# Channel shuffle of 64 MiB: loads and stores in turn on one DMA queue in place of a queue for each

## The chip, the cores and the metric

One core of a Trainium2 chip runs the kernel; the other cores are idle. The metric is the device time of one execution in microseconds (us), median over fast runs. Ratios are from the fast runs of both kernels in the same rounds, so not quite the ratio of the medians quoted. The experiments came in three groups, each on one chip with its own runs of the kernel before (medians 317.56, 317.75 and 316.95 us); compare within a group, and between groups by these ratios only. In the third group the seven runs of the kernel before fall into two sets, 316.8 to 317.0 and 317.6 to 317.9 us, so a ratio of that group is uncertain by some 0.2%.

## The reference

```python
# x: (16, 64, 64, 256) float32, groups = 8, 32 channels in each
x = x.reshape(batch, h, w, groups, channels_per_group)
x = x.transpose(0, 1, 2, 4, 3)
x = x.reshape(batch, h, w, c)
```

Each row of 256 floats is permuted in itself. 67.11 MB are read and 67.11 MB are written; there is no arithmetic.

## The kernel before

```python
_SIZES = [4, 4, 8] + [24] * 20 + [16]     # rows per partition of each tile, 1 KB a row
_IN_BUFS = 4
_OUT_BUFS = 4
...
    for q in _SIZES:
        in_tile = in_pool.tile([P, biggest * c], F32, name="in_tile")
        nc.sync.dma_start(out=in_tile[:, : q * c], in_=rows(x_flat, first, q))
        out_tile = out_pool.tile([P, biggest * c], F32, name="out_tile")
        nc.vector.tensor_copy(
            out=out_tile[:, : q * c].rearrange("p (i j g) -> p i j g", j=CPG, g=G),
            in_=in_tile[:, : q * c].rearrange("p (i g j) -> p i j g", g=G, j=CPG),
        )
        nc.scalar.dma_start(out=rows(out_flat, first, q), in_=out_tile[:, : q * c])
        first += P * q
```

Twenty-four tiles go through four input and four output buffers. SyncE issues all loads on its queue, VectorE copies each tile with the channels permuted, and ScalarE issues all stores on its own queue. Most tiles have 24 KB in each of 128 partitions, 3.146 MB.

Of the kernel before, what the change touches and what calls it, by code (L numbers as in the profile page):

```python
# [1 line left out]

# [4 lines left out]


F32 = mybir.dt.float32
P = 128  # L10

_SIZES = [4, 4, 8] + [24] * 20 + [16]
_IN_BUFS = 4
_OUT_BUFS = 4


@with_exitstack
def kernel(
    ctx: ExitStack,
    tc: tile.TileContext,  # L20
    x: bass.AP,
    groups: bass.AP,
    out: bass.AP,
):
    nc = tc.nc
    b, h, w, c = x.shape
    G = int(groups)
    CPG = c // G
    assert G * CPG == c
    assert sum(_SIZES) * P == b * h * w  # L30
    biggest = max(_SIZES)

    x_flat = x.rearrange("b h w c -> (b h w c)")
    out_flat = out.rearrange("b h w c -> (b h w c)")

    in_pool = ctx.enter_context(tc.tile_pool(name="in_pool", bufs=_IN_BUFS))
    out_pool = ctx.enter_context(tc.tile_pool(name="out_pool", bufs=_OUT_BUFS))

    def rows(flat, first, q):

        return flat[first * c : (first + P * q) * c].rearrange("(p f) -> p f", p=P)

    ctx.enter_context(tc.manual_schedule(engines=None))
    first = 0
    for q in _SIZES:
        in_tile = in_pool.tile([P, biggest * c], F32, name="in_tile")
        nc.sync.dma_start(out=in_tile[:, : q * c], in_=rows(x_flat, first, q))
        out_tile = out_pool.tile([P, biggest * c], F32, name="out_tile")
        nc.vector.tensor_copy(  # L49
            out=out_tile[:, : q * c].rearrange("p (i j g) -> p i j g", j=CPG, g=G),  # L50
            in_=in_tile[:, : q * c].rearrange("p (i g j) -> p i j g", g=G, j=CPG),
        )
        nc.scalar.dma_start(out=rows(out_flat, first, q), in_=out_tile[:, : q * c])
        first += P * q


# [1 line left out]
_INS = ['x', 'groups']  # L58
_OUTS = [((16, 64, 64, 256), 'float32')]

_NUMBERS = {'groups': 8}


# [26 lines left out]
```

## Time and profile before

| | before |
|---|---|
| time, median | 317.67 us (317.63 to 317.87) |
| span of the profiled run | 315.2 us |
| VectorE busy | 122.2 us, 39% |
| queue q1 (loads), share of 16 engines' span | 49.9% |
| queue q10 (stores) | 49.5% |

How to read it: the two queue rows are shares of the time of the same 16 DMA engines, so they add up to 99.4%. The lines are shown in the prediction. Two more lines of the page:

```profile
GB/s 316 399 458 407 423 424 446 430 421 446 437 415 446 437 418 443 440 415 443 440 415 443 443 412 443 446 409 443 446 415 437 446 415 437 443 420 431 431 437 319
...
HBM read 67.11 MB, written 67.11 MB: 426 GB/s over the span
```

The first line is the rate in 40 equal slices of 7.9 us. (The profiled execution of this kernel was a quick one: it took 317.02 us.)

### The profile page before, as it was taken

To read this page: it belongs to the slowest core of one execution; us is meant where nothing else is said; L and a number is where in the kernel's file an instruction comes from. 1 tells how busy PE (TensorE), PEld (TensorE's weight loads), DVE (VectorE), ACT (ScalarE), POOL (GpSimd) and SP (SyncE) were. 2 spreads that over 40 slices of the span, in tenths; PEclk is the share of its full clock that TensorE was granted. 3 is DMA by queue.
4 is the path that set the end of the run, shared out by engine and by line. 5 is a ranking of instruction groups with operands and counts; after the bars stand their busy time and mean duration, and the time that the engine had idled before them with its cause. 6 is when DMAs were issued, how large, how long until landed. Compare 5 with 4: busy or idle time off the path is not lost.

```text
span 315.2 us, 178 instructions
## 1 busy us (share of the span) xinstructions
DVE 122.2 (39%) x24; POOL 0.2 (0%) x4
## 2 busy tenths in 40 slices
DVE  2277517070625335260707162442517070625400
POOL 0000000000000000000000000000000000000000
DMA  8999999999999999999999999999999999999997
GB/s 316 399 458 407 423 424 446 430 421 446 437 415 446 437 418 443 440 415 443 440 415 443 443 412 443 446 409 443 446 415 437 446 415 437 443 420 431 431 437 319
DMA packets 6912, 134.22 MB, mean 426 GB/s; under 512 B 768, under 2 KB 768, under 8 KB 1280
## 3 DMA queue, kind: packets, MB, share of 16 engines
q1 hardware_dynamic: 3456, 67.11, 49.9%
q10 hardware_dynamic: 3456, 67.11, 49.5%
HBM read 67.11 MB, written 67.11 MB: 426 GB/s over the span
## 4 chain that ended last, share of the span: by engine, by line
DMA 38%; another core or an unknown queue 30%; DVE 25%; issue 0%; DVEq 0%
DMA in_tile<-in_x_dram 38%; DVE out_tile L49 25%; DVEq L49 0%
## 5 line engine op out<-in xcount | busy, mean ns | idle before, releaser
L49 DVE COPY out_tile<-in_tile 128x6144 f32<-128x6144 f32 (+3 forms) x24 | 122.2, 5093 | 175.9 <-DMA in_tile<-in_x_dram 175.7
L71 POOL MEMSET const-bfloat16-1.0<- 128x1 bf16 x1 | 0.1, 101 | 0.0
L71 POOL MEMSET const-uint8-127<- 128x1 uint8 x1 | 0.1, 101 | 0.0
L71 POOL MEMSET const-float32-0.0<- 128x1 f32 x1 | 0.1, 98 | 0.2 <-issue 0.2
L71 POOL MEMSET const-float32-1.0<- 128x1 f32 x1 | 0.1, 98 | 0.0
## 6 DMA issues: line engine op xcount, KB each, us to landing
in_tile<-in_x_dram SPq DMA_DIRECT2D x20, 3072.0 KB, 52.3
out_dram<-out_tile ACTq DMA_DIRECT2D x20, 3072.0 KB, 40.1
in_tile<-in_x_dram SPq DMA_DIRECT2D x1, 2048.0 KB, 49.9
out_dram<-out_tile ACTq DMA_DIRECT2D x1, 2048.0 KB, 16.3
in_tile<-in_x_dram SPq DMA_DIRECT2D x2, 512.0 KB, 3.8
in_tile<-in_x_dram SPq DMA_DIRECT2D x1, 1024.0 KB, 6.2
out_dram<-out_tile ACTq DMA_DIRECT2D x2, 512.0 KB, 16.8
out_dram<-out_tile ACTq DMA_DIRECT2D x1, 1024.0 KB, 27.1
```

The lines of the kernel that those rows point to most:

```text
L49: nc.vector.tensor_copy(out=out_tile[:, : q * c].rearrange("p (i j g) -> p i j g", j=CPG, g=G), in_=in_tile[:, : q * c].rearrange("p (i g ...
L71: nc = _bacc.Bacc("TRN2", target_bir_lowering=False, num_devices=1)
```

## The change

The intent: keep the DMA engines fed from one queue in an exact order, store of tile t and then load of tile t + 4, so that ScalarE is free. The tile sizes and the copies stay. The diff, cut to its core:

```diff
-        nc.sync.dma_start(out=in_tile[:, : q * c], in_=rows(x_flat, first, q))
+    def load(t):
+        q = _SIZES[t]
+        in_tiles[t] = in_pool.tile([P, biggest * c], F32, name="in_tile")
+        nc.sync.dma_start(
+            out=in_tiles[t][:, : q * c], in_=rows(x_flat, firsts[t], q)
+        )
+
+    for t in range(_IN_BUFS):
+        load(t)
+    for t, q in enumerate(_SIZES):
 ...  (tensor_copy as before)
-        nc.scalar.dma_start(out=rows(out_flat, first, q), in_=out_tile[:, : q * c])
-        first += P * q
+        nc.sync.dma_start(
+            out=rows(out_flat, firsts[t], q), in_=out_tile[:, : q * c]
+        )
+        if t + _IN_BUFS < len(_SIZES):
+            load(t + _IN_BUFS)
```

More of the change, by code (lines that the diff above doesn't have):

```diff
@@ L43 @@
     ctx.enter_context(tc.manual_schedule(engines=None))
-    first = 0
-    for q in _SIZES:
-        in_tile = in_pool.tile([P, biggest * c], F32, name="in_tile")
-        nc.sync.dma_start(out=in_tile[:, : q * c], in_=rows(x_flat, first, q))
+    firsts = [P * sum(_SIZES[:t]) for t in range(len(_SIZES))]
+    in_tiles = {}
+    def load(t):
[7 more added lines that the diff above has]
+    for t, q in enumerate(_SIZES):
+        in_tile = in_tiles.pop(t)
         out_tile = out_pool.tile([P, biggest * c], F32, name="out_tile")
```

## The prediction

> **What bounds the kernel now.** I read the page in this order: engine shares, the DMA row of the 40 slices, the queues, the costliest groups, the DMA issues. The first three already name the limit.
>
> ```profile
> DVE 122.2 (39%) x24; POOL 0.2 (0%) x4
> ...
> DMA  8999999999999999999999999999999999999997
> ...
> DMA packets 6912, 134.22 MB, mean 426 GB/s; under 512 B 768, under 2 KB 768, under 8 KB 1280
> ...
> q1 hardware_dynamic: 3456, 67.11, 49.9%
> q10 hardware_dynamic: 3456, 67.11, 49.5%
> ```
>
> VectorE, the only engine that computes, works 39% of the 315.2 us span. The 16 DMA engines are busy in every slice; loads (q1, issued by SyncE) and stores (q10, issued by ScalarE) together take 49.9 + 49.5 = 99.4% of their time. So there is no idle DMA time to win, only a different rate per byte. I asked for that rate in stretches (columns: stretch, length, engines' busy time, clock, DMA share, GB/s):
>
> ```profile
> 4.00:6.00 2.00, 1.74 (x2) 0.00 (x0) 1.00 1.05 428
> ...
> 60.00:90.00 30.00, 11.42 (x2) 0.00 (x0) 1.00 1.00 433
> 100.00:200.00 100.00, 39.40 (x7) 0.00 (x0) 1.00 1.00 433
> 306.00:312.00 6.00, 0.00 (x0) 0.00 (x0) 1.00 1.01 431
> ```
>
> From 60 to 200 us both queues run and the rate is 433 GB/s. At 4 to 6 us only loads have started (one queue), at 306 to 312 us only stores are left (the other queue): 428 and 431. Thus **one queue alone, in one direction, fills all 16 engines**; a second queue adds no rate. (Stretches of 2 us are uncertain by some per cent, as packets are booked whole.)
>
> The packet records of the trace say the same: a 24,576-byte packet takes 912 ns, the median on q1 and on q10 alike. Sixteen engines at 24,576 B per 912 ns make 431 GB/s. The completion packets of 4 bytes take 9 ns each. In the store-only end the records show all 16 engines at work across the borders between stores.
>
> The floor: sum the packets by their usual times, 5120 x 912 ns + 512 x 159 (4 KB) + 256 x 309 (8 KB) + 256 x 611 (16 KB) + 768 x 9 = 4993 us; over 16 engines 312.1 us. The first packet starts 2.0 us into the span and the last ends at 314.3 us: 312.4 us of work. The kernel stands on its floor; the measured median of 317.67 is 2.5 us above the span and is taken as fixed.
>
> Now the slack of the copies and the timing of the queue:
>
> ```profile
> 0.73 243.81 SPq L47 DMA_DIRECT2D in_tile<-in_x_dram  x24
> ...
> 209.35 5.67 DVE L49 COPY out_tile<-in_tile 128x6144 f32<-128x6144 f32 x1 [8.82 <-DMA in_tile<-in_x_dram]
> 223.89 5.72 DVE L49 COPY out_tile<-in_tile 128x6144 f32<-128x6144 f32 x1 [8.87 <-DMA in_tile<-in_x_dram]
> ...
> 294.24 3.86 DVE L49 COPY out_tile<-in_tile 128x4096 f32<-128x4096 f32 x1 [6.47 <-DMA in_tile<-in_x_dram]
> ```
>
> Copies start 14.54 us apart (223.89 - 209.35), take 5.7, and wait 8.8 for a load. 14.54 us is two 3.146 MB transfers at 433 GB/s (7.27 us each): the pace is DMA bandwidth, not the copy. Section 6 of the page adds the backlog:
>
> ```profile
> in_tile<-in_x_dram SPq DMA_DIRECT2D x20, 3072.0 KB, 52.3
> out_dram<-out_tile ACTq DMA_DIRECT2D x20, 3072.0 KB, 40.1
> ```
>
> A load lands 52.3 us after its issue, 3.6 periods: transfers sit in the queue long before they run. The chain of waits also names "another core or an unknown queue" for 30%; these pieces of 8.7 us lie exactly where the next load is awaited, so I read them as loads too.
>
> **What the Trainium skill says.** "DMA: Bandwidth & Descriptors", section "Issuing engines are not separate DMA queues": DMAs started by different engines run on the same 16 DMA engines and interleave; several issuers save only issue time. The trace agrees (433 with two queues, 431 with one). Its section "Where 436 GB/s comes from" puts a ceiling of 435 GB/s at the SBUF ports and says that for HBM transfers some 358 GB/s bind; here 433 is held for hundreds of microseconds, so this trace agrees with the first and not the second. Its section "Queues, rings and completion order" says each DMA engine takes turns between its queues packet by packet, and that within a queue descriptors start in order. The records fit: from 60 us on q1 and q10 each have about half of the packets in any stretch.
>
> **The change, part by part.**
>
> 1. *Stores leave ScalarE's queue.* 24 issues of 0.36 us (median 361 ns) go away there. ScalarE does nothing else: worth 0.
>
> 2. *SyncE issues 48 DMAs in place of 24.* At 328 ns each, 2 x 0.33 = 0.66 us per 14.54 us period, while the backlog is tens of us: 0 on the path, except that in the pair (store t, load t+4) the load is issued 0.33 us later than now. Also hidden.
>
> 3. *SyncE waits for copy t before store t, so load t+4 sits behind that wait.* With 4 input buffers, load t+4 writes the buffer that copy t reads, so it had to wait for copy t already. Nothing new.
>
> 4. *The queue becomes first in, first out:* ... S(t-4), L(t), S(t-3), L(t+1), S(t-2), L(t+2), S(t-1), L(t+3), then S(t), L(t+4). When L(t) lands, six transfers are behind it: 6 x 7.27 = 43.6 us. Copy t takes 5.7 us, then two more are added. Lowest backlog: 43.6 - 5.7 = **about 38 us, the queue never runs dry**. Output buffers: copy t needs S(t-4), which stands ahead of L(t), so it is done. Start: when L3 lands near 15 us, S0, L4, S1, L5, S2, L6 (11.5 MB, 26.6 us) are queued, and copy 3 needs 5.7. End: after L23, S20 to S22 (9.44 MB, 21.8 us) remain while copy 23 needs 3.9. No gap at either end.
>
> 5. *Alternation.* Now each DMA engine changes direction at nearly every packet and still does 912 ns per packet. On one queue it changes every 8 packets (128 rows over 16 engines). About 40 changes in place of several hundred: if a change had a price, the kernel before would pay it more often. I put 0 to +0.5 us for what this argument may miss.
>
> 6. *Bytes, packet sizes, copies:* unchanged.
>
> Sum: 0 + 0 + 0 + 0 + about 0.2, so 317.67 becomes about **317.8 us**.
>
> **The rivals.**
>
> A. *The direction change inside one queue has a price.* With two queues, the other's packet can fill any hole while a completion waits for its data; in one queue the load behind a store cannot be overtaken. Same-direction borders show no hole (store-only end, 431 GB/s), but a border between store and load within one queue occurs nowhere in this trace. Being 2% (6.4 us) slower needs 6.4 / 40 = 0.16 us of hole per change on all engines. At 0.05 us it makes 319.7; at 0.3, 330. I give this most of what is left.
>
> B. *Loads win a head start.* Now small stores share turns with big loads at the start; in order, a load has all engines for 7.3 us. L23 then lands with 9.44 + 2.10 MB = 11.5 MB still to write (26.6 us), so its copy starts near 287 us rather than at 294.24. But it only exchanges store time for load time; all bytes still pass at 433. Worth 0. A real gain would need the head (2.0 us), the tail (0.9) or the some 0.3 us over the floor: 1% in all, so faster by 2% is nearly excluded.
>
> C. *The queue's depth runs out.* Up to 8 transfers, 8 x 9 = 72 packets per engine counting completions, wait in one queue where q1 now has four loads (36). If it cannot hold them, SyncE blocks on issue. Against a loss: even half the entries are over 20 us of work. It would show as long issues, not as time.
>
> **Range and chances.** Runs agree within 0.1% (317.63 to 317.87). Downward I allow the head's loss, some 1.3 us: 316.4. Upward 0.09 us per change, 40 x 0.09 = 3.5 us: 321.3. Slower by over 2% needs rival A at nearly twice that: 0.06. Faster by 2% (below 311.3) would lie under the floor of 312.1 plus the head: 0.01. Within 2%: 0.93.
>
> **What would show it.** One queue with all 134.22 MB at about 99% of the 16 engines; 433 GB/s from 60 to 280 us; copies still 14.54 us apart with 8.8 us of idle before each. From issue to landing: a load is issued 5.75 us after L(t) landed and lands 4 periods after it, 58.2 - 5.75 = 52.4 us, as now; a store lands one transfer earlier, 45.1 us (now 40.1). Last copy near 287 us. If the rate falls below 433 with the queue never dry and the period grows beyond 14.6 us, rival A is true and step 5 was wrong; if DVE idles on output buffers, or the DMA row shows slices below 9 in the middle, step 4 was wrong; if issues take microseconds, rival C.

## The result, and the profile after

The changed kernel takes **321.24 us** (320.20 to 321.51, 4 runs) against 317.76 us for the kernel before in the same rounds. The ratio is 1.0107 (95% interval 1.0087 to 1.0128): 1.1% slower, clear of noise, but within 2%. The profiled span went from 315.2 to 319.4 us.

The page of the changed kernel, the lines that answer to those of before:

```profile
DVE 121.7 (38%) x24; POOL 0.2 (0%) x4
...
GB/s 293 366 444 429 442 412 440 428 443 428 419 437 440 434 422 431 431 443 428 419 434 437 437 422 422 443 440 428 419 437 437 443 416 431 437 428 432 437 428 173
...
q1 hardware_dynamic: 6912, 134.22, 98.4%
...
in_tile<-in_x_dram SPq DMA_DIRECT2D x20, 3072.0 KB, 52.1
out_dram<-out_tile SPq DMA_DIRECT2D x20, 3072.0 KB, 45.2
```

One queue now carries everything. From issue to landing a load takes 52.1 us and a store 45.2, as foretold (52.4 and 45.1), so the queue has the order and the backlog that were worked out. But the last slice of the rate row fell from 319 to 173. The stretches show where the rate is lost. First the kernel before (columns: stretch, length, VectorE, GpSimd, clock, DMA share, GB/s):

```profile
60.00:200.00 140.00, 56.56 (x10) 0.00 (x0) 1.00 1.00 433
200.00:280.00 80.00, 29.01 (x6) 0.00 (x0) 1.00 1.01 433
306.00:312.00 6.00, 0.00 (x0) 0.00 (x0) 1.00 1.01 431
312.00:316.00 4.00, 0.00 (x0) 0.00 (x0) 1.00 0.32 135
316.00:320.00 4.00, 0.00 (x0) 0.00 (x0) 1.00 0.00 0
```

Then the changed kernel, the same stretches:

```profile
60.00:200.00 140.00, 56.77 (x10) 0.00 (x0) 1.00 1.00 431
200.00:280.00 80.00, 28.59 (x6) 0.00 (x0) 1.00 1.00 432
306.00:312.00 6.00, 0.00 (x0) 0.00 (x0) 1.00 0.98 419
312.00:316.00 4.00, 0.00 (x0) 0.00 (x0) 1.00 0.60 258
316.00:320.00 4.00, 0.00 (x0) 0.00 (x0) 1.00 0.06 25
```

The middle lost only 0.2 to 0.5%. At the end there is a tail: from 316 to 320 us 6% of the DMA engines' time is used, as much as one engine of 16. So the DMA engines no longer stop together. The page gives the same hint: 98.4% of 319.4 us is 314.3 us of work per engine on average, 99.4% of 315.2 was 313.3. On average an engine has 1.0 us more to do, but the kernel ends 4.2 us later.

The trace records when each of the 16 DMA engines completed its share of every transfer. For the last transfer (us from the span's start, engines sorted by time):

```
                 first   11th    last    spread (last - first)
before           313.72  314.01  314.43  0.71
after            314.23  314.64  318.56  4.33
```

**Eleven of 16 engines end nearly as early as before (0.6 us later); five are late, the last by 4.1 us.** The spread is the time from the first engine's completion of a transfer to the last engine's; a transfer has landed when all 16 have finished, so the last engine sets the time. The copies wait for it too. From the timelines, the last copy of before started at 294.24 us. The last two of the changed kernel:

```profile
279.81 5.71 DVE L59 COPY out_tile<-in_tile 128x6144 f32<-128x6144 f32 x1 [8.81 <-DMA in_tile<-in_x_dram]
292.01 3.87 DVE L59 COPY out_tile<-in_tile 128x4096 f32<-128x4096 f32 x1 [6.49 <-DMA in_tile<-in_x_dram]
```

The first engine completed this last load at 287.55 us, where the prediction had put the copy ("near 287 us"); the last engine came 4.34 us later, at 291.89, and released the copy 0.12 us after that.

**When do engines fall behind?** The spread of a transfer, as it grows in the changed kernel:

```
landing of (first engine)   7.5   15.9  50.2  57.3  86.4  173.6  314.2 us
spread                      1.91  2.09  1.86  2.73  3.14  4.13   4.33 us
```

Two pieces stand out: some 2 us at the head, before the first store has moved, and some 2.3 us between 50 and 174 us (after that the last eight steps from a load to a store add only 0.2). For the second piece I looked at single packets. A 24,576-byte packet takes 912 ns. After 40 us the changed kernel has 43 such packets that took over 930 ns; the kernel before has none. (Before 40 us both kernels have some, 50 and 66; this count leaves the head out.) All 43 lie at the moments when the queue goes over from a load to the following store. Packets of one engine follow each other without a gap, so the records can be sorted into 16 chains. **All 43 stretched packets are on the five engines that end late, and none on the eleven others.** On the two last engines they cost 2.0 and 2.2 us in sum after 43 us; that is the growth of the spread after the head. Three engines around the end of load 7 (durations in ns, the completion packet of the load as |time in us|):

```
on time:  912 912 912 |56.94| 912 912 912 912 912 912
late:     912 912 912 1312 912 |59.34| 912 912 912      (1312 starts at 57.12)
late:     912 912 912 1594 912 |59.66| 912 912 912      (1594 starts at 57.17)
```

While the engine on time has begun to store (after 56.94), the two late ones still load, and there their packet stretches by 0.4 and 0.7 us. No stretched packet lies at the 17 borders where a store is followed by a load.

### The profile page after: what moved, and what is told of

It is laid out like the page before. It is cut to its first block, busy times and chain, and to the rows that moved or that the text cites. A ratio compares the mean times of both kernels' runs of the same rounds, so it can differ in the third digit from the quotient of the medians.

```text
span 319.4 us, 157 instructions
## 1 busy us (share of the span) xinstructions
DVE 121.7 (38%) x24; POOL 0.2 (0%) x4
## 3 DMA queue, kind: packets, MB, share of 16 engines
q1 hardware_dynamic: 6912, 134.22, 98.4%
## 4 chain that ended last, share of the span: by engine, by line
DMA 41%; another core or an unknown queue 28%; DVE 23%; SPq 0%; issue 0%; DVEq 0%
DMA in_tile<-in_x_dram 41%; DVE out_tile L59 23%; SPq L63 0%; DVEq L59 0%; SPq L50 0%
## 6 DMA issues: line engine op xcount, KB each, us to landing
in_tile<-in_x_dram SPq DMA_DIRECT2D x20, 3072.0 KB, 52.1
out_dram<-out_tile SPq DMA_DIRECT2D x20, 3072.0 KB, 45.2
```

## The experiments

At the start there were one theory and several rivals. **Borders:** each step from loads to stores in a queue sets some DMA engines back, and the last engine sets the time. **Rivals:** a cost per transfer on a single queue or of SyncE's 48 issues; a mere chance stall at the head; a price of in-order alternation in a queue whatever else runs. "Stretched" below means a 24,576-byte packet over 930 ns after 40 us (70 us where the queue ran dry at the head).

### The changed kernel again (after_again)

No edit.

> The changed kernel unaltered, for a second trace. In its first trace 11 of 16 DMA engines finish as early as in the kernel before and 5 lag; the slowest lags 4.3 us, of which 1.9 us arose before 8 us and 2.4 us later, in stretched load packets at the moments when the other engines go over from a load to a store. Theory B (border theory: a load still running on a lagging engine is slowed when the others begin to write): 320 to 321.6 us again, stretched 24,576-byte packets again within 3 us of the ends of loads and none at the ends of stores. Theory H (the whole loss is a chance stall at the head of that one run): no growth of the spread after 20 us this time.

Measured: 321.41 us (320.95 to 321.80) against 317.56, ratio 1.0122. Spread 1.4 us at 8 us, 1.1 at 16 us, 4.32 at the end. Of 35 stretched packets 32 lie at the 18 borders from load to store, none at the 17 from store to load. Sorted into chains, 31 of the 35 are on the four engines that end late, and they cost the two last ones 2.4 and 2.5 us. So it was no chance stall of one run: the growth after 20 us repeats, here 3.2 us of it.

### Fewer borders: groups of 2 and of 4

```diff
-        if t + _IN_BUFS < len(_SIZES):
-            load(t + _IN_BUFS)
+        if t % 2 == 1:                       # groups_of_4: t % 4 == 3
+            for u in range(t + _IN_BUFS - 1, t + _IN_BUFS + 1):   # ... - 3
+                if u < len(_SIZES):
+                    load(u)
```

> One queue, but two stores, then two loads: half as many borders from load to store (about 10), the same 48 transfers and packets. Theory B: the part of the lag that grows after 20 us (2.4 us) halves to about 1.2; time about 320 us. Rival S (a cost per transfer on a single queue, or SyncE's 48 issues): as the changed kernel, 321.2. Rival H (head stall only): 321.2 less or more by chance, no link to the borders.

> One queue, four stores, then four loads: a quarter of the borders (about 5). Theory B: growth of the lag after 20 us about 0.6 us, time about 319.4. Rival S: 321.2. The queue stays fed: four stores (29 us) cover the 5.7 us of the last copy of a group, so copies should not cost anything.

Measured: groups_of_2 took 321.56 us (ratio 1.0126), groups_of_4 323.19 us (1.0184). Both numbers miss what the border theory expected.

Groups of 2: 31 of 32 stretched packets lie at its 9 borders from load to store, none between two loads (9 places) or two stores (11), one at a border from store to load. So the *place* is confirmed with another pattern. But the end spread is 4.77 us, not smaller: a border cost more here. The loss is not proportional to the number of borders.

Groups of 4: I had overlooked the head. The third slice of its rate row is the fault:

```profile
DMA  7969999999999999999999999999999999999997
GB/s 303 354 257 391 422 428 422 398 434 440 434 434 428 431 425 440 437 434 425 431 425 440 437 428 431 434 425 437 437 428 431 428 431 437 437 419 435 437 437 313
```

Loads 4 to 7 wait behind store 3, which waits for copy 3, while only three small stores are left in the queue: it runs dry for some 3.5 us. This lets all engines start level (spread 0.59 us at 33 us), and the spread is still 0.77 us at the end; the last slice is back at 313. The run speaks against a cost of 48 issues or of one queue as such making engines late: here both are unchanged and the engines stay level, over five borders. It also shows that a packet can stretch where no border is: between 59.9 and 61.6 us 28 packets did, on all 16 engines (0.4 to 1.1 us each), while the queue was working on load 7 alone; store 4 stood behind it. In dry_once_then_alternate below 34 did at the same place. The counts of these two runs, which start at 70 us, leave these packets out; I have no explanation for them.

### Both queues, each alternating (queue_by_parity)

```diff
+    def queue(t):
+        return nc.sync if t % 2 == 0 else nc.scalar
...
-        nc.sync.dma_start(      # load and store of tile t
+        queue(t).dma_start(
```

> Even tiles' load and store on SyncE's queue, odd tiles' on ScalarE's: each queue still alternates loads and stores in order, but every DMA engine takes packets of two queues in turn, so engines do not all change direction at one moment. Theory B: about as the kernel before, 317.7 to 318.5. Rival F (an order of loads and stores within a queue has a price in itself, whoever else runs): 321 or more.

Measured: 321.55 us (ratio 1.0134), end spread 4.18 us. All 47 stretched packets lie around the ends of loads. My expectation of 318 failed, because I had not thought about phase: the two queues take turns packet by packet with the same contents, so both load, then both store, and the landings come in pairs. What it does show: **a second queue does not help if both carry loads and stores in the same phase; "one queue" is not the cause in itself.**

### Only the small stores, or only the large ones, on the second queue

```diff
-        nc.sync.dma_start(                      # the store
+        (nc.scalar if t < 3 else nc.sync).dma_start(     # small_stores_on_act
+        (nc.sync if t < 3 else nc.scalar).dma_start(     # big_stores_on_act
```

> The changed kernel with only the three small first stores on ScalarE's queue; the 21 others stay on SyncE's. Theory B2 (loss in two parts: some engines are set back 1.1 to 1.7 us before 16 us, then lagging engines are set back further at the borders from load to store, and the last engine ends the kernel): if the small stores in SyncE's queue cause the first part, the spread at 16 us falls to about 0.4 us as before, and with little lag the borders cost little: about 318.5. If they don't cause it: 321.3 as the changed kernel.

> The reverse: the three small stores on SyncE's queue, the 21 others on ScalarE's. From 24 us on loads and stores have a queue each, as in the kernel before. Theory B2: spread of 1 to 2 us at 16 us, no growth after it: 318.8 to 319.5. Rival F1 (all of the loss comes from the first 16 us): 321.3. Rival F2 (all of it from in-order alternation later): 317.6.

Measured: small_stores_on_act 321.02 us (320.01 to 323.11, ratio 1.0113), big_stores_on_act 319.09 us (ratio 1.0041, 1.0023 to 1.0058).

With the small stores on the second queue the spread at 8 us is still 1.54 us, although up to 6 us the instructions are those of the kernel before and packets already stretch from 4.7 us on. So the small stores do not cause the setback at the head. The spread then grows as usual, to 4.65 us.

With the 21 large stores on the second queue, most of the loss is gone. After 90 us there is not one stretched packet; the end spread is 2.06 us, of which 1.57 was there at 16 us. (Between 49 and 81 us 57 packets stretched; they are not at borders of the alternating kind, and I have no explanation.) The rest, 0.4%, fits an engine that carries its setback from the head to the end. With two queues the spread of one queue's landings alone is not the lag: from 83 us on the loads land 3.9 us apart here and the large stores 0.8, so some engines are late with loads and early with stores; the end counts.

### Level engines, then borders (dry_once_then_alternate)

```diff
+        if t == 3:
+            for u in range(_IN_BUFS, 2 * _IN_BUFS):
+                load(u)
-        if t + _IN_BUFS < len(_SIZES):
+        if t > 3 and t + _IN_BUFS < len(_SIZES):
             load(t + _IN_BUFS)
```

> The changed kernel, but loads 4 to 7 wait until store 3 is issued, after that store and load in turn again. The queue runs dry once near 19 to 24 us (3.5 us lost, as in groups_of_4), which lets all DMA engines start level (spread 0.6 us there). Theory B2 (a border costs only an engine that lags): the spread stays under 1 us to the end with some 16 borders, time 317.6 + 3.5 + about 1 = 322. Rival F (each border sets some engines back, level or not): the spread grows to 2 us or more, time 324 or more.

Measured: 326.25 us (ratio 1.027). The spread is 0.60 us at 32 us, as wanted, and then grows: 0.99 at 92, 1.86 at 121, 3.03 at 164, 4.41 us at the end; 32 of 33 stretched packets lie at load-to-store borders. This decides against my theory in the form "a border costs only an engine that already lags": **level engines are pulled apart as well.** The head lag is not needed.

### Large tiles first, on one queue and on two

```diff
-_SIZES = [4, 4, 8] + [24] * 20 + [16]
+_SIZES = [24] * 21 + [8]
```

> One queue in turn as in the changed kernel, but tile sizes 21 x 24 KB and 8 KB at the end in place of small ones first. The queue is full from the start, and four loads of one size run before the first store. Theory B2: if the setback of some engines at the head comes from the borders between small transfers, the head spread is 0.5 us and the borders cost little: 318. Rival F: 320.5 or more, spread growing at the borders all the same.

> The kernel before with tile sizes 21 x 24 KB and 8 KB at the end; loads on SyncE's queue, stores on ScalarE's. Control for big_first (322.85), whose engines started level and ended 5.9 us apart. Theory B3: no borders within a queue, so no growth: 317 to 317.8. If the sizes themselves cost: 321 or more.

Measured: big_first (loads and stores in turn on one queue) 322.85 us, ratio 1.0160 to the kernel before; big_first_two_queues (the same sizes, loads on one queue and stores on the other) 317.68 us, ratio 1.0011 (0.9994 to 1.0029). This is the cleanest pair, though its two runs come from different groups and chips; by the ratios they are 1.5% apart. With large tiles first the head is calm and the engines are within 0.65 us of each other at 10 us in big_first. Then:

```
landing of (first engine)    10.0  47.5  91.1  134.8  178.4  222.0  314.1 us
spread, big_first            0.65  1.04  3.18  3.78   4.67   5.12   5.85 us
```

In big_first all 50 stretched packets lie at the 18 load-to-store borders, none at the 18 store-to-load borders; all 50 are on four engines, and they cost the two last ones 4.2 and 4.5 us. In big_first_two_queues there is one of 931 ns, and the end spread is 1.04 us. First big_first, the rate in 40 slices, then the control:

```profile
GB/s 312 435 429 389 407 435 432 435 438 423 426 432 432 435 435 423 429 432 432 435 438 426 426 432 429 441 438 413 435 435 429 438 435 417 438 421 439 432 426 97
```

```profile
GB/s 305 436 398 423 426 445 429 420 448 429 420 445 439 417 439 442 417 436 445 423 426 445 432 417 448 436 417 442 442 414 439 442 426 426 442 432 423 425 451 285
```

The rows are alike but for the last slice, 97 against 285: a few late engines at work. The control does not beat the kernel before, either.

### The kernel before again (before_again)

No edit.

> The kernel before, for a trace on the chip where the experiments run. In its first trace the engines are within 0.5 us of each other at 8 us and the last ends 0.7 us after the first. Theory B3 (each border from load to store in a queue that all engines share sets some engines back): the end spread is under 1 us again. If engines are set back 1 to 2 us at the head here too, that part of the loss belongs to the chip or the run and not to the change.

Measured: 317.48 us (2 runs). The spread is 1.57 us at 8 us here, so **engines are set back at the head in the unchanged kernel too**; that piece does not come from the change alone. At the end the spread is 1.03 us: much of the setback is still there, but nothing was added to it. From 50 to 269 us the spread of every landing store is 1.19 to 1.21 us (of every load from 63 us on 2.85 to 2.86), and there are no stretched packets after 40 us.

### Two queues in opposite phase (parity_opposite)

```diff
-_SIZES = [4, 4, 8] + [24] * 20 + [16]     # in queue_by_parity
+_SIZES = [24, 12] + [24] * 19 + [20]
```

> As queue_by_parity (321.55), but sizes 24, 12, then 24, which put the two queues in opposite phase: while one loads, the other stores, so every DMA engine reads and writes in turn all the time, as in the kernel before, although each queue alternates in order. Theory B3 in the form that it takes all engines going over from pure loads to pure stores: 317.5 to 318.5, end spread under 1.5 us. Rival F (an order of load then store within a queue costs whatever the other queue does): 320.5 or more.

Measured: 320.73 us (ratio 1.0107), end spread 3.98 us, 29 of 32 stretched packets around the ends of loads. But the trace shows that **the edit did not do what it was for**. The turns between the queues go by packets, not by bytes: the 12 KB packets of tile 1 alternated one for one with the 24 KB packets of tile 0, so the two queues stayed in phase. Loads of both queues land 0.2 us apart (first engine at 112.93 and 113.15 us), then stores of both (127.65 and 127.86). So this run only repeats queue_by_parity, and the question whether opposite phases would avoid the loss is open.

### Few borders without the dry head (groups_of_4_big_first)

```diff
 # groups_of_4 with
+_SIZES = [24] * 21 + [8]
```

> One queue, four stores then four loads, sizes 21 x 24 KB and 8 KB, so that the queue does not run dry at the head. Five borders from load to store in place of some 18 in big_first (322.85, spread growing from 0.65 to 5.9 us). Theory B3: about a quarter of that growth, time 318 to 319. Rival S (a cost of a single queue or of 48 issues by SyncE): 322.85 as big_first.

Measured: 325.28 us (ratio 1.0252), a miss by its time. Again a dry queue, this time at the end:

```profile
274.60 1.86 SPq L50 DMA_DIRECT2D in_tile<-in_x_dram  x2
304.83 7.64 DVE L59 COPY out_tile<-in_tile 128x6144 f32<-128x6144 f32 x2 [30.65 <-DMA in_tile<-in_x_dram]
310.56 2.29 SPq L63 DMA_DIRECT2D out_dram<-out_tile  x2
```

The last two loads stand at the end of the queue; nothing is left behind them, and the last two stores are issued only at 310.56 us. From 306 to 312 us the rate is 68 GB/s. The spread before this gap is the useful number: 0.87 us at 17 us, 2.7 us at 304 us after five borders, against 5.8 us after some 18 in big_first. Fewer borders, less growth, but again not in proportion.

## Why the prediction was right or wrong

The number holds: 321.24 us lies inside 316.4 to 321.3, at the upper edge, and "within 2%" was right. That the range holds is partly luck: the median lies 0.06 us below its upper end, and two of the four runs (321.31 and 321.51) and the median of the repetition (321.41) lie above it. The centre, 317.8 us, was 3.4 us too low. Step by step:

- **Bandwidth is the bound, one queue can fill all 16 engines:** right. The middle runs at 431 to 432 GB/s on one queue.
- **Steps 1 to 4 and 6 (issue time, waits, backlog):** right. Both times to landing were met within 0.3 us, no slice of the DMA row in the middle falls below 9, and no issue took over 0.7 us.
- **Step 5, alternation, "I put 0 to +0.5 us for what this argument may miss": this term was mis-sized.** The measured difference is 3.5 us. The argument was that each engine already changes direction at nearly every packet. That is true of the kernel before and does not carry over: there no queue goes from a load to a store, and no packet stretches after 40 us. With one queue in turn the two last engines lost 2.0 and 2.2 us in stretched packets at borders, on top of some 2 us from the head. The engines drifted apart in every run where a queue carries whole loads and then whole stores, except groups_of_4, whose engines stayed level over five borders; they did not drift after the head where each direction had its own queue throughout. With the same sizes it is 322.85 us (ratio 1.0160) against 317.68 us (ratio 1.0011).
- **Rival A was the right one to fear, but its shape was wrong.** I thought of a hole on all engines at each change, 0.09 us at the edge of the range. The completions exclude that: 11 of 16 engines lost some 0.6 us. A few engines, the same five throughout, lose up to 0.7 us in a packet at a border, and what they lose adds up; only where the queue ran dry did the engines become level again. So the sum over a mean engine (1.0 us) says little; the slowest engine (4.1 us) says all.
- **The signs named beforehand worked.** I had written that a period over 14.6 us with a queue never dry would prove rival A and refute step 5. From 60.13 to 279.81 us there are 15 periods of 14.65 us, against 14.54. The last copy came at 292.0 in place of 287, though the first engine was there on time. (The periods grow because a copy waits for the last engine.)
- **The floor of 312.1 us** assumed that all engines end together, and I took its sum divided by 16. That holds for the kernel before (0.7 us apart) and not after.
- **Small slips in the working,** none of which moves the result: the 2.5 us above the span compares a median with the span of another execution, which took 317.02 us, so it is 1.8 us; 40 x 0.09 is 3.6, not 3.5; the first and last packet, given as 2.0 and 314.3 us, are at 1.7 and 314.1 us in the time of the profile's views.

What is shown: the loss sits in a few late engines; they fall behind after 20 us in stretched packets at steps from load to store, always the same four or five in the three traces that were sorted by engine; giving each direction a queue removes this growth. What is not settled: the head piece of 1 to 2 us appears in the kernel before as well (1.57 us in before_again, 0.46 in the first trace), so how much of it the change makes is open. Nor is it settled why packets stretch at borders, or why on these engines. That writes of the other engines slow the loads of the late ones fits the moments, but no run separated it from something within the engine's own queue, as parity_opposite failed to put the queues out of phase; and the stretch near 60 us in groups_of_4 came without any write. And the cost of one border varies: groups_of_2 lost as much with 9 as the changed kernel with 18.

## What to carry to other kernels

In a kernel bound by DMA bandwidth, give loads and stores a queue each, so that every DMA engine mixes both directions all the time, rather than let all traffic run in long phases of one direction, on one queue or on two; here, on one core, this was worth 1.1 to 1.5%. When busy shares and rates look unchanged and the time still grows, look at the completions engine by engine: the last of the 16 sets the time, and a setback once taken may stay to the end. When you reorder a queue, check its head and its tail for a moment when it runs dry; both of my grouped orders lost microseconds there.

## What the Trainium skill lacked or had wrong

- "DMA: Bandwidth & Descriptors", section "Rules for kernel authors": spreading DMAs over several issuing engines for bandwidth "Doesn't help" and only saves issue time. Here it helped by how loads and stores were divided: with equal sizes 317.68 us (ratio 1.0011 to the kernel before) with a queue for each direction and 322.85 us (1.0160) with both in turn on one, while issue time was hidden in both. What it saved was not rate but the late engines at the end. A second queue with loads and stores on each, in the same phase, brought nothing (321.55 us).
- The same page, section "Where 436 GB/s comes from": some 358 GB/s is said to bind HBM transfers, without a condition; this core, alone, held 433 GB/s from 60 to 280 us. (Elsewhere the page gives this figure for both cores of a pair at work, which no run here tests.)
- No page has it that a few of the 16 engines can fall further and further behind over a kernel when loads and stores take turns in a queue: at the end they were 4.3 us apart in the changed kernel and 5.9 us with large tiles first, against 0.7 to 1.0 us with a queue for each direction.
- No page says what taking turns by packets means for packets of unlike size: 12 KB and 24 KB packets alternated one for one here, and two queues stayed in phase (landings 0.2 us apart).
- "Perfetto Trace Analysis", section "DMA Optimizations", says that separate engines for inputs and outputs may make sense, above all with loops, "to allow more dynamic spread", without a number; here it was worth 1.1% (changed kernel) to 1.5% (large tiles first).
